# Encoder trunk on one core: operands of the first down steps made during the last gate/up pair, and a new order of the down products

## The chip, the cores and the metric

One core of a Trainium2 chip runs the whole program. The metric is the device time in microseconds (us), median of the runs; lower is better.

## What is computed

One layer of an encoder for 256 prompt and 1024 sample tokens (1280 together, width 1024): RMSNorm, an input projection, two groups of attention, an output projection added to the residual, and a feed-forward block. The change lies in the feed-forward block:

```
h2 = rmsnorm(x, ffn_norm_g)
x = x + (silu(h2 @ w_gate) * (h2 @ w_up)) @ w_down      # w_gate, w_up: 1024 x 2816; w_down: 2816 x 1024
y = rmsnorm(x, final_norm_g)
```

All is float32. TensorE multiplies in `float32r`, so every operand is split into a high part (a cast on ScalarE, called ACT in the profile) and a low part (raw minus high, on VectorE, DVE, or on GpSimd, POOL), and `mm3` issues three matmuls: high by high, high by low, low by high (lines 110 to 112).

## The kernel before

**Gate and up.** Both products are done block by block with seven products of half blocks instead of eight (a Strassen scheme). The tokens are in two halves of `NQ` = 640, the features in halves. Eleven pairs `fp` of output tiles are worked through; in each, first the gate (`i` = 0, into `G`), then the up part (`i` = 1, into `U`), each with the products `m` in the order `SEQ = (1, 2, 6, 7, 4, 5, 3)`. `S[m]` is the split activation operand of a product (TensorE's moving side, "S" and "zA" in the trace), made once for all pairs; `operand` makes the weight operand `wc` of each product (ACT and POOL, lines 849 and 850). `product` runs 24 matmuls of 320 columns, in two halves `s`, into the PSUM tiles `M0` and `M1`, and DVE adds each result into `G` or `U` (line 922). Products 2, 4 and 3 go on in the PSUM tile of the product ahead of them (`CHAIN`), once DVE has read it. `finish` applies Silu to a finished part of `G`, multiplies it into `U` (line 939), and makes the seven activation operands of the down projection (line 950), which are stored to `act_d[m][fp]` in DRAM. In the last pair these stores go through POOL's queue (`store_p`, line 70), in earlier pairs through ACT's.

**Down.** Again seven products, in the order `SEQ2`, each over `NH` = 11 steps `f`. A step needs an activation operand (loaded as `as` from `act_d[m][f]`, split into `ah`) and a weight operand (loaded as `w0_f` and `w1_f`, for the two halves of the columns; where `B_OP[m]` names two blocks they are first added or subtracted into `ws` on DVE, line 1065; then split into `w`). Both splits are `split_f`, lines 1025 (ACT) and 1026 (DVE). A step has 15 matmuls of 512 columns (5 token tiles by `mm3`) into the PSUM tiles `d`. After the last step of a product, `put` adds its five tiles into the output rows `x5` (`xs`, loaded from `xm_d`), one DVE instruction for each block that `D_OUT[m]` names (lines 1075 and 1077). `prepare`, `final` and `final_half` do the last RMSNorm.

**What sets the order.** SyncE's queue (SP), which issues all loads, keeps the order of the code; the other engines are ordered by a scheduler when the program is built. The down loop calls `bring` (loads) four steps ahead and `fetch` (splits) two steps ahead. Memory comes from stacks of pools: when the gate/up pools are released, the down pools take their place, and a tile in a reused place waits until the tile that was there has been read for the last time. Before, `x5` lay over the buffers `z` (the last pair's `G` and `U`), the raw down weights over `S7` and `S4`, the split weights `w` over `S6`.

## Time and profile before

| | us |
|---|---|
| median of 3 runs | 1669.48 |
| the runs | 1664.52, 1669.48, 1670.19 |
| the profiled execution, its own time | 1666.5 |
| its span, first to last instruction | 1664.5 |
| TensorE busy with matmuls | 1604.7 (96% of the span) |
| VectorE, ScalarE, GpSimd busy | 883.8, 716.7, 659.3 |
| mean granted TensorE clock | 0.992 |

The profile covers one execution. Its span runs from the first to the last instruction, and 2.0 us of that execution's time lie outside it. Gate and up end at 1376.5 us of the span, the down projection follows, and the last matmul begins at 1655.90. TensorE is busy nearly everywhere, so the places to look at are those where it waits or where its granted clock is under 1.00. In a timeline, the second number is how long an instruction (or a run of x equal ones) took; matmuls overlap, so the distance between two starts is what one costs.

### The profile page before, as it was taken

The page shows a single profiled execution, that of the slowest core. Times are in us where ns is not written, and L with a number is a line of the kernel's source. Part 1 is how long each engine was busy: PE and PEld are TensorE (multiplying, and loading weights), DVE is VectorE, ACT ScalarE, POOL GpSimd, SP SyncE. Part 2 cuts the span into 40 slices and gives each one's busy share as a digit, 9 for nine tenths or more (in the row PEclk, how much of TensorE's full clock was granted, in tenths as well). Part 3 has the DMA queues.
Part 4 walks back from the last instruction along what each step waited for, and adds up shares of the span by engine and source line. Part 5 has one row for each costly group of instructions (what it writes and reads, how often), then busy time and mean ns, then how long its engine had stood idle before and what let it go on. Part 6 is the DMA issues. An engine that isn't in the chain of part 4 may idle for free.

```text
span 1664.5 us, 25614 instructions
## 1 busy us (share of the span) xinstructions
PE 1604.7 (96%) x9601; PEld 1448.6 (87%) x9601; DVE 883.8 (53%) x1473; ACT 716.7 (43%) x1480; POOL 659.3 (40%) x803
## 2 busy tenths in 40 slices
PE   7999999999899999999989999999999999999998
PEld 6987899987688888788889999999999997788886
DVE  4654045455677777533464444334444437755776
ACT  5534145454577777544353222233223223333434
POOL 3451435354011119224677656565665550000101
PEclk9999999999999999999999999999999999999999
DMA  6635302225001003234302332232232228633434
GB/s 211 216 99 149 75 21 61 36 95 167 20 19 34 20 30 99 77 108 152 121 23 95 102 107 81 66 100 86 94 107 94 78 88 330 242 92 91 151 100 150
DMA packets 123212, 170.04 MB, mean 102 GB/s; under 512 B 35345, under 2 KB 66961, under 8 KB 123089
## 3 DMA queue, kind: packets, MB, share of 16 engines
q1 hardware_dynamic: 78848, 119.25, 23.0%
q10 hardware_dynamic: 43680, 46.87, 8.2%
q0 software_dynamic: 560, 2.29, 0.4%
q8 instruction: 75, 1.23, 0.3%
q14 instruction: 49, 0.39, 0.1%
HBM read 117.91 MB, written 50.46 MB: 101 GB/s over the span
## 4 chain that ended last, share of the span: by engine, by line
PE 82%; issue 4%; DMA 4%; DVE 4%; ACT 3%; POOL 3%; SPq 1%; ACTq 0%; POOLq 0%; DVEq 0%
PE M L110 11%; PE M L112 11%; PE M L111 11%; PE d L111 4%; PE d L112 4%; PE d L110 4%; PE o L686 3%; PE tp L679 3%; PE po L110 2%; PE po L111 2%; PE na_o L462 2%; PE po L112 2%; PE pj L110 2%; PE pj L112 2%; PE pj L111 2%
## 5 line engine op out<-in xcount | busy, mean ns | idle before, releaser
L110 PE MATMUL M<-S,wc 128*128 128x320 f32 x1056 | 322.4, 310 | 5.3 <-ACT wc L849 5.2
L111 PE MATMUL M<-S,wc 128*128 128x320 f32 x1056 | 324.9, 309 | 0.0
L112 PE MATMUL M<-S,wc 128*128 128x320 f32 x1056 | 313.2, 310 | 0.0
L110 PEld LDWEIGHTS M<-S,wc 128*128 128x128 f32 x1056 | 198.4, 189 | 5.9 <-ACT wc L849 5.8
L111 PEld LDWEIGHTS M<-S,wc 128*128 128x128 f32 x1056 | 199.3, 189 | 0.0
L112 PEld LDWEIGHTS M<-S,wc 128*128 128x128 f32 x1056 | 195.7, 189 | 0.6 <-POOL wc L850 0.6
L850 POOL TENSOR_TENSOR wc<-A,wc 128x512 fp32r<-128x512 f32 x86 | 119.5, 1391 | 83.6 <-ACT wc L849 83.2
L111 PE MATMUL d<-w,ah 128*128 128x512 f32 x385 | 147.1, 400 | 2.5 <-DVE w L1026 2.5
L110 PE MATMUL d<-w,ah 128*128 128x512 f32 x385 | 142.9, 400 | 2.7 <-ACT ah L1025 2.7
L112 PE MATMUL d<-w,ah 128*128 128x512 f32 x385 | 145.0, 400 | 0.0
L922 DVE TENSOR_TENSOR z<-M,z 128x320 f32<-128x320 f32 x120 | 56.9, 488 | 142.4 <-PE M L112 121.4
L849 ACT CAST wc<-A 128x512 fp32r<-128x512 f32 x86 | 53.5, 622 | 167.7 <-PE M L111 132.3
L850 POOL TENSOR_TENSOR wc<-sum,wc 128x512 fp32r<-128x512 f32 x62 | 88.3, 1425 | 86.6 <-ACT wc L849 81.5
L922 DVE TENSOR_TENSOR zB<-M,zB 128x320 f32<-128x320 f32 x100 | 47.6, 488 | 133.0 <-PE M L112 116.3
L100 DVE TENSOR_TENSOR PT<-tp,PT 128x512 fp32r<-128x512 f32 (+1 forms) x144 | 93.1, 658 | 41.1 <-ACT PT L99 39.7
L1025 ACT CAST ah<-as 128x640 fp32r<-128x640 f32 x77 | 56.0, 727 | 121.8 <-issue 61.9
L849 ACT CAST wc<-sum 128x512 fp32r<-128x512 f32 x62 | 38.4, 619 | 149.4 <-PE M L111 101.1
L99 ACT CAST PT<-tp 128x512 fp32r<-128x512 f32 (+1 forms) x144 | 79.2, 565 | 42.4 <-PE tp L679 39.4
L1026 DVE TENSOR_TENSOR ah<-as,ah 128x640 fp32r<-128x640 f32 x77 | 64.2, 836 | 53.9 <-ACT ah L1025 53.9
L110 PEld LDWEIGHTS d<-w,ah 128*128 128x128 f32 x385 | 73.2, 190 | 21.2 <-ACT ah L1025 3.4
L671 DVE TENSOR_REDUCE mm<-S 128x1 f32<-128x1024 f32 (+1 forms) x80 | 84.8, 1061 | 12.7 <-PE S L112 11.0
L111 PEld LDWEIGHTS d<-w,ah 128*128 128x128 f32 x385 | 73.1, 190 | 20.7 <-DVE w L1026 2.9
(398 smaller groups left out, 3978.0 us busy)
## 6 DMA issues: line engine op xcount, KB each, us to landing
as<-act_d SPq DMA_DIRECT2D x77, 320.0 KB
act_d<-z ACTq DMA_DIRECT2D x35, 320.0 KB
act_d<-zB ACTq DMA_DIRECT2D x35, 320.0 KB
A<-in_w_gate_dram SPq DMA_DIRECT2D x42, 256.0 KB
A<-in_w_up_dram SPq DMA_DIRECT2D x42, 256.0 KB
x<-in_x_tm_dram SPq DMA_DIRECT2D x20, 512.0 KB
cT_d<-stg ACTq DMA_DIRECT2D x20, 320.0 KB
w<-in_w_down_dram SPq DMA_DIRECT2D x11, 512.0 KB
```

Source lines behind the costliest of these rows:

```text
L99: i = nc.scalar.copy(out=hi, in_=ps)
L100: nc.vector.tensor_sub(out=lo, in0=ps, in1=hi)
L110: nc.tensor.matmul(out, lhsT=sh, rhs=mh, start=first, stop=False, **kw)
L111: nc.tensor.matmul(out, lhsT=sh, rhs=ml, start=False, stop=False, **kw)
L112: return nc.tensor.matmul(out, lhsT=sl, rhs=mh, start=False, stop=last, **kw).ins
L671: nc.vector.reduce_max(out=nm[:, u:u + 1], in_=S, axis=AX.X, negate=True)
L679: nc.tensor.transpose(tp[:, j], ex[:, kt * P:(kt + 1) * P], ident)
L849: i0 = nc.scalar.copy(out=hi, in_=raw)
L850: i1 = nc.gpsimd.tensor_tensor(out=lo, in0=raw, in1=hi, op=ALU.subtract)
L922: nc.vector.tensor_add(out=o, in0=ps, in1=a)
L1025: nc.scalar.copy(out=o[:, 0], in_=raw)
L1026: nc.vector.tensor_sub(out=o[:, 1], in0=raw, in1=o[:, 0])
```

## The change

- `S[1]` and `S[2]` become one tile each (`[P, 2, 4, NQ]`, high and low together) in the pool `rS`; the pool `rC` is gone, and `rS` is released at the very end.
- New: `down_first`, called in the last pair behind product 2 of the up part, when `S1` and `S2` are read for the last time. It takes their two places as rings, five slots for down weights (`w_ring`) and four for down activations (`a_ring`), and makes the operands of the first `EARLY` = 3 down steps in them: three weight tiles are loaded into buffers `A11`, `A12`, `A11` of the gate/up weights, three activation tiles into a buffer `zB`, and each is split by `split_f`.
- The down loop uses these rings for all steps (a fifth slot `ah` for the activations is new in `r5b`), skips what is made already, and has the order `SEQ2 = (5, 3, 1, 6, 2, 4, 7)` instead of `(3, 6, 1, 5, 2, 4, 7)`. Product 5 needs one weight block, `22`, and no sum.
- The output rows `xs` are loaded otherwise: five whole ones in product 5 (it writes only these), the halves of the other five in products 3 and 1. `gl_b` is loaded at the end of product 5, and `prepare` follows product 3.
- The pools `l5x`, `l5r` and those of the right side move: `x5` of row 0 now lies over `S6`, those of rows 1 to 5 over `z`, the raw down weights over `S5` and `S7`.
- In the first pair, `finish(G, U, i, 2, fp)` with the first Silu is called at `m == 4` instead of `m == 6`.

```diff
-    rC = pool("rC", side="right")
-    S = {1: [rS.tile([P, 4, NQ], F32R, name="S1", bufs=2) for x in "hl"],
-         2: [rC.tile([P, 4, NQ], F32R, name="S2", bufs=2) for x in "hl"]}
+    S = {}
+    for m in (1, 2):
+        x = rS.tile([P, 2, 4, NQ], F32R, name=f"S{m}")
+        S[m] = [x[:, 0], x[:, 1]]
...
+    def split_f(o, raw):
+        nc.scalar.copy(out=o[:, 0], in_=raw)
+        nc.vector.tensor_sub(out=o[:, 1], in0=raw, in1=o[:, 0])
+
+
+    NH = NF // 2
+    EARLY = 3
+    ops, w_ring, a_ring = {}, [], []
+
+    def down_first():
+        ring = rS.tile([P, 5, 2, 512], F32R, name="S1")
+        w_ring.extend(ring[:, n] for n in range(5))
+        ring = rS.tile([P, 4, 2, NQ], F32R, name="S2")
+        a_ring.extend(ring[:, n] for n in range(4))
+        z = rB.tile([P, 4, NQ], F32, name="zB", bufs=2)
+        for f in range(EARLY):
+            raw = rY.tile([P, 4, P], F32, name=("A11", "A12", "A11")[f],
+                          bufs=1 if f == 1 else 2).rearrange("p a b -> p (a b)")
+            load(raw, w_down[2 * f + 1 + NF])
+            load(z[:, f], act_d[5][f])
+            split_f(a_ring[f], z[:, f])
+            split_f(w_ring[f], raw)
+            ops[5, f] = a_ring[f], w_ring[f]
+
...
-                    if m == 6:
+                    if m == 4:
                         finish(G, U, i, 2, fp)
...
+                    if m == 2 and i == 1 and fp == NF // 2 - 1:
+                        down_first()
...
-    rC.release()
...
-    l5w, l5x, l5r = l5 = [pool("l5w"), pool("l5x"), pool("l5r")]
+    l5x, l5r = l5 = [pool("l5x"), pool("l5r")]
...
+    a_ring.append(r5b.tile([P, 2, NQ], F32R, name="ah"))
...
-        h = r5b.tile([P, 2, NQ], F32R, name="ah", bufs=5)
+        h = a_ring[steps.index((m, f)) % 5]
...
-        w = l5w.tile([P, 2, 512], F32R, name="w", bufs=5)
+        w = w_ring[steps.index((m, f)) % 5]
...
-    SEQ2 = (3, 6, 1, 5, 2, 4, 7)
+    SEQ2 = (5, 3, 1, 6, 2, 4, 7)
...
     def fetch(m, f):
-        ops[m, f] = act_operand(m, f), w_operand(m, f)
+        if (m, f) not in ops:
+            ops[m, f] = act_operand(m, f), w_operand(m, f)
...
-        load_a(m, f)
-        for n in (f - 2,) if 2 <= f < NH - 1 else (NT - 2, NT - 1) if f == NH - 1 else ():
-            if m == 3:
+        if (m, f) not in ops:
+            load_a(m, f)
+        if 2 <= f < 7 and m in (5, 3, 1):
+            n = f - 2 + (0 if m == 5 else 5)
+            if m != 1:
                 xs[n] = l5x.tile([P, D], F32, name="x5", bufs=10)
-                load(xs[n][:, 512:], xm_d[n][:, 512:])
-            elif m == 6:
-                load(xs[n][:, 0:512], xm_d[n][:, 0:512])
-        if m == 1 and f == 0:
+            cs = {5: slice(0, D), 3: slice(512, D), 1: slice(0, 512)}[m]
+            load(xs[n][:, cs], xm_d[n][:, cs])
+        if m == 5 and f == NH - 1:
             load(gl_b, g_fin.partition_broadcast(P))
...
-                if m == 5:
+                if m == 3:
                     prepare(t, ps[t])
...
+    rS.release()
```

The order of the instructions, as the program is built, is the same in both kernels on every engine up to the last pair. Three places show what that means. **The first Silu, on ACT**, in the first pair, before:

```order
L920 COPY z_9211<-M0_9286 128x320
L937 ACT_TABLE_LOAD
L937 ACTIVATE z_9210<-z_9210 128x640
L813 ACTIVATE zB_8005<-trm_9167,gf_8022 128x128 x4
L920 COPY z_9211<-M0_9272 128x320
```

And after the change:

```order
L921 COPY z_9206<-M0_9281 128x320
L938 ACT_TABLE_LOAD
L938 ACTIVATE z_9205<-z_9205 128x640
L814 ACTIVATE zB_8000<-trm_9162,gf_8017 128x128 x4
L921 COPY z_9206<-M0_9267 128x320
```

Only line and buffer numbers differ; the Silu and the table load ahead of it stand where they stood. **The last pair, on DVE**, from the evacuation of product 2 of the up part on, before (z_14074 is `G`, z_14075 is `U`, and M0_14425 and M1_14439 hold products 7 and 4):

```order
L922 TENSOR_TENSOR z_14075<-M0_14392,z_14075 128x320
L939 TENSOR_TENSOR z_14075<-z_14075,z_14074 128x640
L922 TENSOR_TENSOR z_14075<-M1_14406,z_14075 128x320
L922 TENSOR_TENSOR z_14075<-M0_14425,z_14075 128x320
L922 TENSOR_TENSOR z_14075<-M1_14439,z_14075 128x320
```

And after the change (z_14069 is `G`, z_14070 `U`, M0_14444 and M1_14458 hold products 7 and 4; S1_14378 and S2_14379 are the rings):

```order
L923 TENSOR_TENSOR z_14070<-M0_14411,z_14070 128x320
L968 TENSOR_TENSOR S1_14378<-A12_14388,S1_14378 128x512
L968 TENSOR_TENSOR S1_14378<-A11_14395,S1_14378 128x512
L923 TENSOR_TENSOR z_14070<-M1_14425,z_14070 128x320
L940 TENSOR_TENSOR z_14070<-z_14070,z_14069 128x640
L968 TENSOR_TENSOR S2_14379<-zB_14380,S2_14379 128x640 x2
L923 TENSOR_TENSOR z_14070<-M0_14444,z_14070 128x320
L968 TENSOR_TENSOR S2_14379<-zB_14380,S2_14379 128x640
L923 TENSOR_TENSOR z_14070<-M1_14458,z_14070 128x320
```

Four of the six early low parts now stand between the evacuation of product 2 and that of product 7's first half. On **SP** at the same place, after the change:

```order
L64 DMA A12_14388<-in_w_down_dram 128x512
L64 DMA zB_14380<-act5_d1_107 128x640
L64 DMA A11_14395<-in_w_down_dram 128x512
L64 DMA zB_14380<-act5_d2_108 128x640
L64 DMA w1_0_14605<-in_w_down_dram 128x512
L64 DMA w1_1_14607<-in_w_down_dram 128x512
L64 DMA w1_2_14609<-in_w_down_dram 128x512
L64 DMA x5_14611<-xm_d0_139 128x1024
L64 DMA w1_3_14613<-in_w_down_dram 128x512
L64 DMA as_14615<-act5_d3_109 128x640
L64 DMA x5_14617<-xm_d1_140 128x1024
L64 DMA w1_4_14619<-in_w_down_dram 128x512
```

The loads of steps 0 to 3 now stand ahead of x5_14617, the first load that goes into a place of `z`; before, x5_14602 in such a place stood behind the loads of steps 0 to 2 and ahead of those of step 3. **The end of the first down product, on DVE**, before (d_14640 to d_14644 are its results; w_14928 with ah_14923 is the operand of step 12, the second of the next product):

```order
L1065 TENSOR_TENSOR ws_14926<-w0_1_14863,w1_1_14594 128x512
L1026 TENSOR_TENSOR ah_14895<-as_14838,ah_14895 128x640
L1075 TENSOR_TENSOR x5_14602<-d_14640,x5_14602 128x512
L1075 TENSOR_TENSOR x5_14722<-d_14640,x5_14722 128x512
...
L1065 TENSOR_TENSOR ws_14964<-w0_2_14890,w1_2_14598 128x512
L1026 TENSOR_TENSOR ah_14923<-as_14865,ah_14923 128x640
...
L1075 TENSOR_TENSOR x5_14811<-d_14644,x5_14811 128x512
L1026 TENSOR_TENSOR w_14928<-ws_14926,w_14928 128x512
```

And after the change (ws_14839, ws_14865 and ws_14901 become the weights of steps 11, 12 and 13):

```order
L1086 TENSOR_TENSOR ws_14839<-w1_0_14605 128x512
L968 TENSOR_TENSOR S1_14378<-ws_14839,S1_14378 128x512
L1086 TENSOR_TENSOR ws_14865<-w1_1_14607 128x512
L968 TENSOR_TENSOR S2_14379<-as_14789,S2_14379 128x640
L1086 TENSOR_TENSOR ws_14901<-w1_2_14609 128x512
L968 TENSOR_TENSOR S2_14379<-as_14811,S2_14379 128x640
L968 TENSOR_TENSOR S1_14378<-ws_14865,S1_14378 128x512
L968 TENSOR_TENSOR S1_14378<-ws_14901,S1_14378 128x512
L1098 TENSOR_TENSOR x5_14611<-x5_14611,d_14625 128x512
L1096 TENSOR_TENSOR x5_14611<-d_14625,x5_14611 128x512
L968 TENSOR_TENSOR S2_14379<-as_14833,S2_14379 128x640
```

Before, the ten additions of `put` stood ahead of step 12's weight; now the weights of steps 11 to 13 stand ahead of all ten.

## Rows read from the trace of the kernel before

**Rows 1.** Page: one of three down groups; count, busy us, mean ns, idle before.

```profile
L111 PE MATMUL d<-w,ah 128*128 128x512 f32 x385 | 147.1, 400 | 2.5 <-DVE w L1026 2.5
```

**Rows 2.** Waits of TensorE, 1340 to 1664.5: us in total, times, longest.

```profile
PE d L110 <- ACT ah L1025: 2.7, 1, 2.7
PE d L111 <- DVE w L1026: 2.5, 1, 2.5
```

**Rows 3.** Timeline of TensorE: start us, us, instruction, idle before and releaser.

```profile
1376.34 0.31 PE L112 MATMUL M<-zA,wc 128*128 128x320 f32 x1
1379.33 0.51 PE L110 MATMUL d<-w,ah 128*128 128x512 f32 x1 [2.68 <-ACT ah L1025]
...
1384.48 1.34 PE L110 MATMUL d<-w,ah 128*128 128x512 f32 x5
...
1390.34 1.33 PE L112 MATMUL d<-w,ah 128*128 128x512 f32 x5
...
1424.38 0.40 PE L110 MATMUL d<-w,ah 128*128 128x512 f32 x1
1427.26 0.50 PE L111 MATMUL d<-w,ah 128*128 128x512 f32 x1 [2.48 <-DVE w L1026]
...
1432.40 0.39 PE L111 MATMUL d<-w,ah 128*128 128x512 f32 x1
...
1655.90 0.40 PE L112 MATMUL d<-w,ah 128*128 128x512 f32 x1
```

**Rows 4.** Windows: stretch, length, busy us of PE, PEld, DVE, ACT, POOL, clock, DMA, GB/s.

```profile
1380.00:1390.00 10.00, 10.00 (x38) 7.98 (x37) 5.99 (x10) 2.50 (x4) 1.08 (x2) 0.83 0.53 183
...
1384.50:1392.00 7.50, 7.44 (x32) 5.72 (x31) 3.49 (x6) 2.50 (x4) 0.00 (x0) 1.00 0.75 257
1400.00:1420.00 20.00, 20.00 (x87) 16.08 (x86) 13.13 (x20) 10.03 (x16) 0.00 (x0) 1.00 1.05 401
...
1429.60:1432.40 2.80, 2.80 (x9) 2.19 (x8) 2.80 (x5) 1.39 (x3) 0.00 (x0) 0.61 0.63 195
1432.40:1500.00 67.60, 67.60 (x290) 54.37 (x289) 43.57 (x65) 25.37 (x41) 0.00 (x0) 1.00 0.45 148
```

**Rows 5.** Timeline of DVE in the last pair and at the start of down.

```profile
1362.02 1.70 DVE L939 TENSOR_TENSOR z<-z 128x640 f32<-128x640 f32 x1 [2.08 <-ACT z L920]
...
1364.37 0.49 DVE L922 TENSOR_TENSOR z<-M,z 128x320 f32<-128x320 f32 x1 [0.25 <-PE M L112]
...
1368.48 0.49 DVE L922 TENSOR_TENSOR z<-M,z 128x320 f32<-128x320 f32 x1 [1.85 <-PE M L112]
...
1376.91 0.49 DVE L922 TENSOR_TENSOR z<-M,z 128x320 f32<-128x320 f32 x1
...
1380.03 0.82 DVE L1026 TENSOR_TENSOR ah<-as,ah 128x640 fp32r<-128x640 f32 x1
...
1389.71 0.69 DVE L1065 TENSOR_TENSOR ws<-w 128x512 f32<-128x512 f32 x1 [2.64 <-DMA w<-in_w_down_dram]
```

**Rows 6.** Timeline of POOL in the last pair.

```profile
1355.83 1.29 POOL L860 TENSOR_TENSOR sum<-A,sum 128x512 f32<-128x512 f32 x1
...
1361.74 1.30 POOL L850 TENSOR_TENSOR wc<-A,wc 128x512 fp32r<-128x512 f32 x1 [3.36 <-ACT wc L849]
```

**Rows 7.** Timeline of ACT in the last pair.

```profile
1361.04 0.62 ACT L849 CAST wc<-A 128x512 fp32r<-128x512 f32 x1 [2.69 <-PE M L111]
```

**Rows 8.** The chain that ended last, 1340 to 1440: start us, us, what.

```profile
1380.41 4.51 DMA act_d<-z
1385.06 0.33 SPq L64
```

**Rows 9.** DMA issues, 1340 to 1400: count, KB each, median us to landing.

```profile
act_d<-z POOLq DMA_DIRECT2D x7, 320.0 KB, 2.8
```

**Rows 10.** Timeline of DVE at the end of the first down product.

```profile
1419.19 3.68 DVE L1075 TENSOR_TENSOR x<-d,x 128x512 f32<-128x512 f32 x6 [2.49 <-PE d L112]
...
1426.51 0.69 DVE L1026 TENSOR_TENSOR w<-ws,w 128x512 fp32r<-128x512 f32 x1
```

More of the change, by code (lines that the diff above doesn't have):

```diff
@@ L1009, in encoder_trunk @@
     rY.release()
-    rS.release()
     pm[1].release()
     pm[0].release()
-    NH = NF // 2
     NLAST = 5
-    l5w, l5x, l5r = l5 = [pool("l5w"), pool("l5x"), pool("l5r")]
+    l5x, l5r = l5 = [pool("l5x"), pool("l5r")]
     r5a, r5b = r5 = [pool(nm, side="right") for nm in ("r5a", "r5b")]
@@ L1022, in encoder_trunk @@
     halves = r5a.tile([P, 5], F32, name="halves")
-    def split_f(o, raw):
-        nc.scalar.copy(out=o[:, 0], in_=raw)
-        nc.vector.tensor_sub(out=o[:, 1], in0=raw, in1=o[:, 0])
+    a_ring.append(r5b.tile([P, 2, NQ], F32R, name="ah"))
     B_OP = {1: ("11", ALU.add, "22"), 3: ("12", ALU.subtract, "22"), 6: ("11", ALU.add, "12"),
@@ L1112, in encoder_trunk @@
              7: (("11", 1),)}
-    SEQ2 = (3, 6, 1, 5, 2, 4, 7)
+    SEQ2 = (5, 3, 1, 6, 2, 4, 7)
     AHEAD, LOADED = 2, 4
     steps = [(m, f) for m in SEQ2 for f in range(NH)]
-    ops = {}
     def fetch(m, f):
-        ops[m, f] = act_operand(m, f), w_operand(m, f)
+        if (m, f) not in ops:
+            ops[m, f] = act_operand(m, f), w_operand(m, f)
     def bring(m, f):
         load_w(m, f)
-        load_a(m, f)
-        for n in (f - 2,) if 2 <= f < NH - 1 else (NT - 2, NT - 1) if f == NH - 1 else ():
-            if m == 3:
+        if (m, f) not in ops:
[3 more added lines that the diff above has]
+            if m != 1:
                 xs[n] = l5x.tile([P, D], F32, name="x5", bufs=10)
-                load(xs[n][:, 512:], xm_d[n][:, 512:])
-            elif m == 6:
-                load(xs[n][:, 0:512], xm_d[n][:, 0:512])
-        if m == 1 and f == 0:
+            cs = {5: slice(0, D), 3: slice(512, D), 1: slice(0, 512)}[m]
+            load(xs[n][:, cs], xm_d[n][:, cs])
+        if m == 5 and f == NH - 1:
             load(gl_b, g_fin.partition_broadcast(P))
```

## The prediction

> **What bounds the kernel now.** I read the page first: matmuls fill 96% of the span, so only places where TensorE waits or runs slowly can give time. The waits of TensorE behind 1340 us then show two, and only two, both in the down projection [rows 2]. The timeline of TensorE places them [rows 3]. The first is the change of stage: the last gate/up matmul starts at 1376.34, the first down matmul at 1379.33, held by the activation operand that ACT makes. The second is at 1424.38, where step 12, early in the second down product, waits 2.48 us for DVE to split its weight. The windows show what follows each: the granted clock is 0.83 over 1380 to 1390 and 0.61 over 1429.6 to 1432.4, against 1.00 later, so part of either stretch ran at 1.2 instead of 2.4 GHz; ahead of both TensorE stood still for some 2.5 us [rows 3, 4].
>
> **What undisturbed work would take.** From 1384.48 to 1390.34 there are five rows of five matmuls, so one costs 5.86 / 25 = 0.2344 us. Three groups of 385 [rows 1] are 1155 matmuls. Started without a gap at 1376.34 + 0.15 = 1376.49, the last would start 1154 x 0.2344 = 270.5 later, at 1647.0, and not at 1655.90: 8.9 us are in play. The parts: gap one 1379.33 - 1376.49 = 2.84; the first step's 15 matmuls took 5.15 instead of 3.52, 1.63 more; gap two 2.88 - 0.23 = 2.65; the 15 matmuls behind it 5.14 instead of 3.52, 1.62 more; 0.2 is scattered over steps 2 and 3. That is the most that this change can bring.
>
> **The change part by part.**
>
> *First Silu.* Nothing: the built order has it, with its table load, where it was. 0.
>
> *One tile for S1 and S2, other places, no pool rC.* Order and work up to the last pair are unchanged; 0.
>
> *Gap one.* Step 0 reads operands made some ten us ahead, so 2.84 goes, and with the standstill the slow stretch, 1.63. What could be late next is PSUM: the last evacuation of gate/up starts at 1376.91 and takes 0.49 [rows 5]. The built program puts the first five `d` tiles in other banks than this one, so I take 0; were one of them there, the second tile (needed 0.7 us after the start, at 1377.19) would wait some 0.3.
>
> *The early operands.* Added in the last pair: six loads, six casts on ACT, six low parts on DVE. DVE pays 3 x 0.69 (128x512, as in [rows 10]) + 3 x 0.82 (128x640 [rows 5]) = 4.5 us. The second weight tile goes into `A12`, which POOL reads until 1355.83 + 1.29 = 1357.1 [rows 6]; the nearest landing, 2.8 us for 320 KB [rows 9], puts it in SBUF at 1360. Its cast (some 0.62, as [rows 7]) is over before 1361.04, when the cast `wc` queued behind it on ACT ran anyway [rows 7]. The third cast follows at 1361.66 and its low part can start on DVE near 1362.3. There POOL is in its own subtraction, from 1361.74 to 1363.04 [rows 6], and DVE's line 939, started at 1362.02, took 1.70 instead of 0.82 [rows 5]: it ended 0.68 behind POOL's. So the low part ends near 1363.7; an evacuation (0.40), line 939 (0.74) and two more low parts (2 x 0.74) carry DVE to 1366.3, and the evacuation of product 7's first half, at 1364.37 before, ends at 1366.8. TensorE wants it for product 4, whose first half is evacuated at 1368.48 [rows 5]: less 12 matmuls of 0.1465 (0.2344 x 320 / 512) and some 0.2 it starts at 1366.5. So 0.3 to 0.4 us of waiting. Bounds: 0 if the low part misses POOL's instruction; 2.2 if both others are held 0.88 as well. I take 0.4, the walk along the rows.
>
> The Trainium skill (SBUF — State Buffer, Who interferes with whom) says that a DVE instruction with two SBUF inputs and a GpSimd instruction that reads SBUF lock each other out for a whole instruction. The 1.70 of line 939 agrees with it. By that rule each of the six low parts can be held, and the page speaks against putting them here; the sum above has one of them held, the second rival three, with its own time.
>
> *The SP queue.* The load of `x5` row 1 now goes into `U`'s place and waits for the last store of `act_d`; behind it stand the loads of step 4. Before, `x5` row 0 waited in the same way, until the store of 1380.41 had landed 4.51 later, at 1385.06 [rows 8], with step 3's loads behind it. In the change the three DVE instructions ahead of the last store follow the evacuation directly: 1376.91 + 0.40 + 3 x 0.83 + 0.3 to POOL = 1380.1; landing 2.8 [rows 9] to 4.5 later, so SP goes on at 1383.0 to 1384.8. Before, 768 KB behind such a release had landed 4.65 later (1385.06 to 1389.71, [rows 5, 8]); row 1's 512 KB and the 256 KB weight are the same 768 KB, and step 4's activations add 320 KB at 401 GB/s [rows 4], 0.8: in at 1388.5 to 1390.3, cast 0.8 later. Step 4 starts at 1376.49 + 60 x 0.2344 = 1390.55. So 0 to 0.6 late; with most landings near 2.8 I take 0.2. Steps 5 to 7 each load 1088 KB, 2.8 us at 401 GB/s, under a step's 3.52, so the delay doesn't grow. Over the whole first product the loads fall from 11 x (512 + 320) + 10 x 256 = 11,712 KB to 11 x 256 + 8 x 320 + 5 x 512 + 512 = 8,448 KB.
>
> *Gap two.* Product 5 has no `ws`: DVE's work for a step falls from 0.69 + 0.69 + 0.82 to 1.5 us. At its end the weights of steps 11 to 13 stand ahead of the ten additions. The next one behind them is step 14's: 10 x 0.61 (3.68 / 6, [rows 10]), 3 splits of activations (3 x 0.74), 2 `ws` and one split (3 x 0.61) are 10.2 us from the first addition; TensorE reaches step 14 three steps, 10.5 us, after the product's end. So 2.65 and 1.62 go, with little to spare; price if not, 4.3.
>
> *The rest.* `put`, `prepare`, `final` and the tail behind 1655.90 have the same instructions; `gl_b` comes earlier. 0. The scattered 0.2 goes too.
>
> **Sum.** 8.9 - 0.4 - 0.2 = 8.3. The span becomes 1664.5 - 8.3 = 1656.2, the profiled execution's 1666.5 becomes 1658.2. That execution lies 3.0 under the median; the four known executions average 1667.7. 8.3 off the median is 1661.2, off the average 1659.4; I predict **1660.3**.
>
> **Rivals.** *Gap two stays, or moves to a later product's end.* For it: 0.3 us of margin in the count above, and ten additions instead of the two-row ones of product 6 at more ends. Against: DMA, at 401 GB/s in 1400 to 1420 [rows 4], was what kept the operands only just ahead, and it has less to do. It gives back 4.3: 1660.3 + 4.3 = 1664.6.
>
> *DVE and POOL in the last pair.* If the low parts that stand ahead of product 7's evacuation are held like line 939 was, 0.88 each, TensorE waits 2.2 instead of 0.4, long enough for the slow stretch behind gap two: 1.8 + 1.6 more, 1663.7. For it the 1.70 in [rows 5]; against it, POOL has only one subtraction between 1361.7 and the store.
>
> *Slower: the loads of steps 4 to 7.* Each of these steps needs 1.11 MB. In 1380 to 1390 the queues moved 183 GB/s [rows 4]. If that were what they can do beside the stores, a step would take 6.1 us instead of 3.52: four steps lose 10.3, with two slow stretches of 1.6 13.5, and 8.3 - 13.5 gives 5.2 more than now, 1674.7. It turns into a loss below about 230 GB/s. Against it: 401 GB/s ten us later, and that the 183 contain SP's standstill until 1385.06.
>
> *The change doesn't do what it says.* True of the Silu (counted as 0). For the early operands the SP order shows their loads ahead of the down loads, so little is left: 1669.5.
>
> **Chances.** Forecast 64%, gap two 17%, DVE and POOL 9%, slower by the loads 5%, nothing gained 5%. A measurement of this kernel tells 0.5% from no change, 8.3 us: exactly the forecast's size. With the spread of the runs (1664.5 to 1670.2) I give five sixths of the forecast to faster, the rest and the next two rivals to the same: faster 0.54, same 0.40, slower 0.06. The range goes from the lowest run less 8.9, 1655.6, over the two rivals near 1664 up to 1667, their times with the runs' spread of 2 to 3.
>
> **What would show it.** Right: no wait between the last `M` and the first `d`, granted clock 1.00 over the first steps, the last `d` starting about 270.6 after the first, SP standing still at `x5` row 1 until about 1384. Wrong: a wait on DVE in the last pair of more than 0.5, on ACT at step 4, or on DVE behind a product's end; then the slow stretch behind it.

## The result, and the profile after

The changed kernel takes 1660.28 us (median of 15 runs, 1652.63 to 1664.00), the kernel before 1669.48 (15 runs beside them, 1664.52 to 1672.73): ratio 0.9941, 95% interval 0.9927 to 0.9954. The time came out where the prediction put it, 1660.3, but not by the sum that the prediction made. One term of that sum was twenty times too small, another that stood at 0 was the largest of all, and the two nearly cancel, so that the time was hit is luck. The experiments take them apart.

The profiled execution took 1656.26 us, its span 1654.4. The page's down group, which answers to [rows 1], has a new shape (activation operands in the ring `S` or in the fifth slot `ah`) and a shorter mean, 390 ns instead of 400:

```profile
L111 PE MATMUL d<-S,S 128*128 128x512 f32 x310 | 120.6, 390 | 0.0
```

The waits of TensorE behind 1340 us, in answer to [rows 2] (us in total, times, longest):

```profile
PE d L110 <- ACT ah L967: 2.8, 1, 2.8
PE M L110 <- DVE z L923: 0.4, 1, 0.4
PE M L110 <- ACT wc L850: 0.3, 1, 0.3
```

Both waits of before are gone. A new one of 2.8 us has come, and two small ones in the last gate/up pair. The timeline of TensorE, in answer to [rows 3], places the new one:

```profile
1377.41 0.31 PE L112 MATMUL M<-zA,wc 128*128 128x320 f32 x1
1377.56 0.39 PE L110 MATMUL d<-S,S 128*128 128x512 f32 x1
...
1390.05 1.29 PE L112 MATMUL d<-S,S 128*128 128x512 f32 x5
1394.15 0.50 PE L110 MATMUL d<-S,ah 128*128 128x512 f32 x1 [2.81 <-ACT ah L967]
...
1399.31 0.39 PE L110 MATMUL d<-S,S 128*128 128x512 f32 x1
...
1645.79 0.39 PE L112 MATMUL d<-S,S 128*128 128x512 f32 x1
```

Gate and up run straight into down (0.15 us apart), but step 4 waits. The windows, in answer to [rows 4] (stretch, length, busy us of PE, PEld, DVE, ACT, POOL, clock, DMA, GB/s):

```profile
1380.00:1390.00 10.00, 10.00 (x46) 8.29 (x45) 2.91 (x4) 1.35 (x2) 1.08 (x2) 1.00 0.72 278
...
1394.15:1398.00 3.85, 3.85 (x11) 3.02 (x12) 1.95 (x3) 1.34 (x2) 0.00 (x0) 0.65 1.04 393
```

The clock is 1.00 where it was 0.83, and 0.65 behind the new standstill: part of that stretch ran at 1.2 GHz.

**Account.** The instructions ahead of the first gate/up matmul are the same in both kernels, so I compare the stretch from that matmul to the last down matmul: 824.90 to 1655.90 before, 825.08 to 1645.79 after, 831.00 against 820.71 us, 10.3 less.

| | predicted | measured |
|---|---|---|
| gap one and the slow stretch behind it, scattered 0.2 | -4.7 | -4.7 |
| gap two and the slow stretch behind it | -4.3 | -4.3 |
| gate and up with the early operands | +0.4 | +0.9 |
| step 4 late | +0.2 | +4.6 |
| pace of the down matmuls | 0 | -6.9 |
| sum | -8.3 (from unrounded terms) | -10.4; the stretch says -10.3 |

Gate and up: first to last matmul 552.33 instead of 551.44. Step 4: 1394.15 less 1390.05 + 5 x 0.2267 is 2.97 of standstill, and its 15 matmuls took 5.16 instead of 3.49, 1.67 more. Pace: the undisturbed down matmuls average 0.2284 us instead of 0.2344, 1155 x 0.0060.

### The profile page after: what moved, and what is told of

It is laid out like the page before. It is cut to its first block, busy times and chain, and to the rows that moved or that the text cites. A ratio compares the mean times of both kernels' runs of the same rounds, so it can differ in the third digit from the quotient of the medians.

```text
span 1654.4 us, 25670 instructions
## 1 busy us (share of the span) xinstructions
PE 1597.0 (97%) x9601; PEld 1448.0 (88%) x9601; DVE 884.3 (53%) x1473; ACT 716.6 (43%) x1480; POOL 663.7 (40%) x803
## 4 chain that ended last, share of the span: by engine, by line
PE 83%; issue 4%; POOL 4%; DMA 3%; ACT 2%; DVE 2%; SPq 1%; POOLq 0%; ACTq 0%; DVEq 0%
PE M L112 10%; PE M L110 10%; PE M L111 10%; PE d L110 5%; PE d L112 5%; PE d L111 5%; PE o L686 3%; PE tp L679 3%; PE po L110 2%; PE po L111 2%; PE po L112 2%; PE pj L110 2%; PE pj L112 2%; PE pj L111 2%; PE na_o L462 2%
## 5 line engine op out<-in xcount | busy, mean ns | idle before, releaser
L111 PE MATMUL d<-S,S 128*128 128x512 f32 x310 | 120.6, 390 | 0.0
L110 PE MATMUL d<-S,S 128*128 128x512 f32 x310 | 118.6, 389 | 0.0
L112 PE MATMUL d<-S,S 128*128 128x512 f32 x310 | 117.2, 390 | 0.0
L699 POOL TENSOR_TENSOR ob<-ob 128x128 f32<-128x128 f32 x40 | 18.4, 461 | 177.0 <-ACT ob L696 176.9
L967 ACT CAST S<-as 128x640 fp32r<-128x640 f32 x59 | 42.9, 729 | 99.0 <-issue 60.1
L679 PE MATMUL tp<-ident,ex 128*128 128x128 f32 x544 | 79.8, 274 | 4.8 <-ACT ex L673 3.4
L686 PE MATMUL o<-PT,v 128*128 128x256 f32 x544 | 81.5, 288 | 1.6 <-ACT PT L99 1.4
```

The lines of the kernel that those rows point to most:

```text
L110: nc.tensor.matmul(out, lhsT=sh, rhs=mh, start=first, stop=False, **kw)
L111: nc.tensor.matmul(out, lhsT=sh, rhs=ml, start=False, stop=False, **kw)
L112: return nc.tensor.matmul(out, lhsT=sl, rhs=mh, start=False, stop=last, **kw).ins
L679: nc.tensor.transpose(tp[:, j], ex[:, kt * P:(kt + 1) * P], ident)
L686: nc.tensor.matmul(oT, lhsT=vv, rhs=pt[s][g][:, j], start=kt == 0 and s == 0, stop=kt == nkt - 1 and s == 1)
L967: nc.scalar.copy(out=o[:, 0], in_=raw)
```

## Why step 4 was late

The chain of the work that ended last shows it (start us, us, what):

```profile
1381.72 6.08 DMA act_d<-z
1387.94 0.33 SPq L64
1388.32 0.42 SPq L64
1388.84 4.46 DMA as<-act_d
1393.38 0.73 ACT ah L967
1394.15 0.50 PE d L110
```

SP's own queue shows the standstill: nothing between the load of step 3's activations and that of `x5` row 1.

```profile
1376.36 0.43 SPq L64 DMA_DIRECT2D as<-act_d  x1
1387.94 0.33 SPq L64 DMA_DIRECT2D x<-xm_d  x1
```

The prediction had this chain, and took its first two links too short: the last store was issued at 1381.72 and not 1380.1, and landed 6.08 us later and not 2.8 to 4.5. The third link it had right: step 4's activations were in 5.4 us behind SP's release at 1387.94, and 5.45 was predicted. So they came at 1393.3 and not at 1388.5 to 1390.3. The landing is the largest miss. Over the stores of this stretch it rose from a median of 2.9 to 7.0 us. What changed beside the stores is the loads: before, SP issued none between 1368.54 and 1385.06; now those of steps 0 to 3, which stand ahead of row 1, move at the same time. The two groups of DMA issues, 1374 to 1388, before and then after (KB each, us to landing):

```profile
act_d<-z POOLq DMA_DIRECT2D x6, 320.0 KB, 2.9
```

```profile
act_d<-z POOLq DMA_DIRECT2D x6, 320.0 KB, 7.0
```

and the loads in the same stretch, before and after (packets, MB, share of 16 engines):

```profile
q1 hardware_dynamic: 418, 0.83, 17.8%
```

```profile
q1 hardware_dynamic: 864, 1.90, 42.1%
```

Two of the runs below agree. With still more loads beside the stores (`rows_apart`, 2.74 MB in 1376 to 1390) their median is 8.3 us. In the run without early operands the four stores beside the loads have a median of 7.9, and the last one, issued when SP had started nothing for eight us, took 3.0.

**Experiment: the rows elsewhere.** Everything of the change is kept but the place of five output rows. The order of the instructions is the same on every engine.

```diff
-                xs[n] = l5x.tile([P, D], F32, name="x5", bufs=10)
+                xs[n] = l5x.tile([P, D], F32, name="x5" if n < 5 else "x6", bufs=5)
```

> The changed kernel with one thing moved: the five output rows of product 5 get a ring of their own over S6 (x5), the other five a ring over z (x6); the order of the instructions is the same on every engine. Theory one: TensorE's wait of 2.81 us at step 4 comes from SP, which stands at output row 1 from 1376.8 to 1387.9 until the last stores out of U have landed (6.08 us for the last one), with step 4's loads behind it. Rows over S6 don't wait for stores: SP goes on at once, no wait on ACT at step 4, granted clock 1.00 there, and the 2.9 of standstill and 1.9 of slow stretch go: span 1654.4 - 4.8 = 1649.6, last d starting 4.8 earlier against the first d. Theory two: the loads of step 4 are late because 1.1 MB a step and the seven stores share the queues, wherever the rows lie: the wait stays at 1 us or more, somewhere in steps 4 to 7, and the span at 1652 to 1655.

It takes 1654.62 us, ratio 0.9908 (0.9879 to 0.9936), and all that is left of the wait in down is

```profile
PE d L110 <- ACT ah L967: 0.2, 1, 0.2
```

First to last down matmul takes 264.09 us instead of 268.23, 4.1 less; the stretch of the account 817.10 instead of 820.71. So theory one holds: the place of the rows made SP wait for the stores, and 4.1 of the 4.8 come back. The profiled span fell less, to 1652.2 and not to 1649.6, because this execution reached its first gate/up matmul 1.4 us later and gate and up took 0.5 longer. What is missing of the 4.8 is theory two in small. SP now issues at once, and the loads pile up: in 1381 to 1393 the queues move 393 GB/s, and the activations of step 4 land 12.47 us after their issue, which makes step 4 0.2 us late.

```profile
1381.00:1393.00 12.00, 12.00 (x55) 9.86 (x53) 4.54 (x6) 2.24 (x4) 1.33 (x3) 1.00 0.99 393
```

## Why the down matmuls became faster

The trace of the changed kernel has a pattern that the prediction didn't foresee: four of five steps take 3.40 to 3.43 us (15 matmuls), the fifth, whose activation operand is in `ah`, 3.49. Before, all took 3.52. These are the first matmuls of four steps in a row, late in down:

```profile
1560.31 0.39 PE L110 MATMUL d<-S,S 128*128 128x512 f32 x1
...
1563.71 0.39 PE L110 MATMUL d<-S,S 128*128 128x512 f32 x1
...
1567.12 0.39 PE L110 MATMUL d<-S,ah 128*128 128x512 f32 x1
...
1570.61 0.39 PE L110 MATMUL d<-S,S 128*128 128x512 f32 x1
```

TensorE waits for nothing there, and its clock is 1.00. What goes by five is the slot, so the place of the operands was the suspect: of which operand, and which property of the place? Four runs of this section, the first two, the one of five more distances and the one of gate and up, are a single execution each (1665.79, 1660.34, 1660.89 and 1660.88 us) and are read for their paces alone.

**Experiment: the activation operand at other places.** The ring's slots are cut out of plain tiles at chosen offsets.

```diff
-        ring = rS.tile([P, 4, 2, NQ], F32R, name="S2")
-        a_ring.extend(ring[:, n] for n in range(4))
+        ring = rS.tile([P, 8 * NQ], F32R, name="S2")
+        a_ring.extend(ring[:, o:o + 2 * NQ].rearrange("p (a b) -> p a b", a=2)
+                      for o in (0, 2 * NQ + 8, 4 * NQ + 48))
...
-    a_ring.append(r5b.tile([P, 2, NQ], F32R, name="ah"))
+    low = r5b.tile([P, 4 * NQ + 56], F32R, name="ah")
+    a_ring.extend(low[:, o:o + 2 * NQ].rearrange("p (a b) -> p a b", a=2)
+                  for o in (0, 2 * NQ + 56))
```

> The changed kernel with the five slots of the activation operand (TensorE's stationary side) at other places; the weight slots (moving side) stay in the S1 ring. Slot 0: byte 208864 of the partition, 32 above a multiple of 64, as it was; slot 1: 214016, a multiple of 64; slot 2: 219296, 32 above; slot 3: 101920, 32 above, in the low region; slot 4: 107264, a multiple of 64, as it was. Step i uses slot i modulo 5, so one profile gives five paces. Theory A, alignment of the stationary operand: 0.2267 us for a matmul in slots 0, 2 and 3, 0.233 in slots 1 and 4. Theory B, region: 0.2267 in slots 0, 1 and 2, 0.233 in slots 3 and 4. Theory C, it is neither but something that goes with the fifth step (the load traffic, the scheduler's order): 0.2267 in slots 0 to 3, 0.233 in slot 4.

Matmuls 15 apart, from slot 0 to the next slot 0:

```profile
1562.29 0.40 PE L112 MATMUL d<-S,S 128*128 128x512 f32 x1
...
1565.72 0.40 PE L112 MATMUL d<-S,S 128*128 128x512 f32 x1
...
1569.21 0.39 PE L112 MATMUL d<-S,S 128*128 128x512 f32 x1
...
1572.65 0.40 PE L112 MATMUL d<-S,ah 128*128 128x512 f32 x1
...
1576.15 0.40 PE L112 MATMUL d<-S,ah 128*128 128x512 f32 x1
...
1579.64 0.40 PE L112 MATMUL d<-S,S 128*128 128x512 f32 x1
```

The steps take 3.43, 3.49, 3.44, 3.50 and 3.49 us. None of the three theories fits: slot 3 is slow though it lies 32 above a multiple of 64 (against A), slot 1 is slow in the upper region (against B), and three slots are slow, not one (against C).

**Experiment: the weight operand at other places.** The same for `w_ring`: offsets 0, 1032 and 2096 columns in `S1`, two slots in the lower region; the fifth activation slot goes into the rest of `S1`.

> The changed kernel with the five slots of the weight operand (moving side) at other places, and all five activation slots in the high region at 32 above a multiple of 64. Weight slot 0: byte 188384, 32 above a multiple of 64, as it was; slot 1: 192512, a multiple of 64; slot 2: 196768, 32 above; slot 3: 103968, 32 above, low region; slot 4: 108288, a multiple of 64, low region. Theory A, alignment of the stationary operand alone: 0.2267 us in all five slots. Theory A2, both operands must lie alike: 0.233 or 0.234 in slots 1 and 4. Theory B, region, of the moving operand too: slower in slots 3 and 4. Before, the moving operand was low, 32 above a multiple of 64, and the stationary one low and a multiple of 64: 0.2344.

The steps take 3.44, 3.50, 3.49, 3.44 and 3.49 us. Theory A falls (slots 1, 2 and 4 are slow), so does B (slot 3 is fast in the lower region), and A2 (slot 2 is slow, though both operands lie 32 above a multiple of 64).

What orders both runs is the distance: start of the stationary operand less start of the moving one, modulo 256 bytes. It is 0, 32, 192, 64 and 32 in the first run, 0, 224, 64, 192 and 224 in the second; 0 and 192 are fast in both, all others slow. Before it was 96. I call this theory D, and it was formed after these two runs, so it needed a test of its own.

**Experiment: the kernel before, shifted by 96 bytes.** One number, on a tile that has nothing to do with it:

```diff
-    halves = r5a.tile([P, 5], F32, name="halves")
+    halves = r5a.tile([P, 29], F32, name="halves")
```

> The kernel before with one number changed: the tile halves has 29 columns instead of 5, so the five activation operands ah lie 96 bytes lower, at 160 modulo 256 like the weight operands w; before they lay at 0. Nothing else changes, neither order nor amount of work. Theory D, from the paces of place_stationary and place_moving: the pace goes by the distance from the moving to the stationary operand modulo 256; 0 and 192 gave 0.2267 to 0.230, 32, 64 and 224 gave 0.232 to 0.2335, and before, at 96, it is 0.2343. So here, at 0, 0.227 to 0.230 in all steps: 1155 x 0.0045 to 0.0076 = 5 to 9 us less, ratio 0.995 to 0.997; both gaps stay. Rival, the rings' place in the upper region is what counts: 0.234 as before, ratio 1.000.

It takes 1659.15 us, ratio 0.9953 (0.9936 to 0.9970). Every undisturbed step takes 3.40 us:

```profile
1552.45 0.39 PE L110 MATMUL d<-w,ah 128*128 128x512 f32 x1
...
1555.85 0.39 PE L110 MATMUL d<-w,ah 128*128 128x512 f32 x1
```

and both gaps of before are still there:

```profile
PE d L110 <- ACT ah L1025: 3.2, 2, 2.7
PE d L111 <- DVE w L1026: 2.7, 1, 2.7
```

So 24 unused columns in the kernel before give nearly all of what the whole change gives: 0.9953 against 0.9941. The region is not the cause; these operands lie where they lay, but for 96 bytes.

**Experiment: five more distances.** The same slots as in the first experiment, at other offsets.

> The changed kernel with five distances of the stationary operand from the moving one, modulo 256: slots 0 to 4 at 128, 160, 192 (upper region), 96 and 0 (lower region). Theory D: slots 2 and 4 at 0.2267 to 0.230, slot 3 at 0.234 (the distance of before), 128 and 160 not measured yet. Rival, region: slots 3 and 4 slow, 0 to 2 fast.

The steps take 3.49 (128), 3.50 (160), 3.44 (192), 3.51 (96) and 3.44 us (0, in the lower region). Both named slots are fast, 96 is the slowest as before, region falls again. All eight multiples of 32 are measured now:

| distance modulo 256 | 0 | 32 | 64 | 96 | 128 | 160 | 192 | 224 |
|---|---|---|---|---|---|---|---|---|
| us per step of 15 | 3.40 to 3.44 | 3.49 | 3.49, 3.50 | 3.51, 3.52 | 3.49 | 3.50 | 3.44 | 3.49, 3.50 |

A fast step beside slow ones reads 3.43 or 3.44, one among fast ones 3.40; 192 was only measured beside slow ones.

**Experiment: the fifth slot at distance 0.** `rows_apart` with `halves` at 13 columns:

```diff
-    halves = r5a.tile([P, 5], F32, name="halves")
+    halves = r5a.tile([P, 13], F32, name="halves")
```

> The kernel rows_apart with the tile halves at 13 columns instead of 5, so the fifth activation slot lies 32 bytes lower, at distance 0 modulo 256 from its weight operand instead of 32. Theory D: the fifth slot's steps go from 0.2327 to 0.2267 to 0.229, 15 steps x 15 x 0.004 to 0.006, with what the steps beside them gain some 1 to 2 us less than rows_apart: about 1653. Rival, the fifth slot is slow because it lies in the lower region: no change, 1654.6.

It takes 1650.59 us, ratio 0.9898 (0.9876 to 0.9919); the fifth steps take 3.40, and first to last down matmul falls from 264.09 to 262.31 us. Theory D holds here too: 1.8 less, as expected.

**Experiment: gate and up.** Their matmuls have 320 columns and take 0.1467 us. The six buffers `wc` were put at three other distances.

```diff
-        hi = rY.tile([P, 4, P], F32R, name="wc", bufs=6)
-        lo = rY.tile([P, 4, P], F32R, name="wc", bufs=6)
+        if not wcs:
+            t = rY.tile([P, 6 * 512 + 128], F32R, name="wc")
+            wcs.extend(t[:, 512 * n + o:512 * n + o + 512].rearrange("p (a b) -> p a b", a=4)
+                       for n, o in enumerate((32, 32, 72, 72, 104, 104)))
+        hi, lo = wcs[0:2]
+        wcs[:] = wcs[2:] + wcs[0:2]
```

> The changed kernel with the three pairs of weight operands wc of gate and up at 128, 32 and 160 bytes further on modulo 256, used in turn by the products. The gate and up matmuls (320 columns) are at 0.1467 us, and their distances are 0 (products 1, 2, 3) and 64 (6, 7, 4, 5) now. Together with the products the three pairs give the distances 128, 192, 32, 96, 160 and 224. Theory D carried over to 320 columns: some of the blocks of 24 matmuls leave 0.1467, by up to 0.005 either way. Rival, these shorter matmuls don't go by the distance: 0.1467 in all blocks.

Next to nothing moves: where TensorE doesn't wait, the blocks of 24 lie between 0.1462 and 0.1472 us, against 0.1463 to 0.1467 in the changed kernel, and the groups' means stay at 309 to 310 ns. With 320 columns the distance makes at most 0.0005 us of difference, and none of the distances is faster than those in use; the 3696 matmuls of gate and up have nothing to gain from it.

Why the distance counts is open. The Trainium skill (SBUF — State Buffer, Who interferes with whom) lists two independent read ports of TensorE, one for the moving operand and one for loading weights, and says "PE and ACT never wait on anyone". The runs don't contradict the part on other engines. But the two sides of TensorE itself are not independent of each other here: the same 512-column matmul costs 0.2267 or 0.2343 us by nothing but the distance of its operands.

## What the early operands bring

**Experiment: without them.** The changed kernel with one number changed.

```diff
-    EARLY = 3
+    EARLY = 0
```

> The changed kernel with EARLY = 0: no operands are made in the last pair, all else is kept (rings, order of the products, places of the rows). Theory one: gap one comes back (about 2.8 us of wait on ACT before the first d, and a slow first step, 1.6 more), but it covers the lateness of step 4, whose loads go on when the last store has landed, near 1387, as before; and the last pair ends about 0.7 to 1.1 earlier. So the span stays within 2 us of 1654.4: in the changed kernel the early operands bring nothing yet. The pace of the d matmuls stays 0.2267 where the activation operand is in the S2 ring and 0.233 in the fifth slot. Theory two: step 4's wait is apart from gap one and comes on top: both are there, span near 1658.9.

It takes 1659.68 us, ratio 0.9944 (0.9926 to 0.9962), which the times don't tell from the changed kernel; by the stretch of the account it is 1.5 us slower (822.19 against 820.71). Neither theory has the reasons right. Gap one comes back as 0.97 instead of 2.99 us, and step 4's wait does not go, it grows:

```profile
1378.12 0.31 PE L112 MATMUL M<-zA,wc 128*128 128x320 f32 x1
1379.09 0.51 PE L110 MATMUL d<-S,S 128*128 128x512 f32 x1 [0.65 <-ACT S L967]
```

```profile
PE d L110 <- ACT ah L967: 4.0, 1, 4.0
PE d L110 <- ACT S L967: 0.8, 2, 0.7
```

The wait at step 4 grows because the last store is issued later. On DVE the low parts of steps 0 to 2 now stand among the last operands for `act_d`, and POOL issues the last store at 1387.80, where it was 1381.72 with early operands; SP went on right behind its landing, at 1390.97 instead of 1387.94.

```profile
1387.80 0.54 POOL L70 DMA_DIRECT2D act_d<-z  x1 [1.78 <-DVE z L951]
```

Two thirds of gap one, however, had gone without any early operand. The traces show why. Before, the first step's weight needed a sum (`ws`, DVE, at 1377.31), and ACT's cast waited for it until 1378.03. In the new order the first product is 5, which needs no sum; ACT's cast starts at 1377.37, as soon as the load is in, with gate and up still running. (This run keeps the new places too; what they do to gap one by themselves it doesn't show.) First the kernel before, then this one (ACT):

```profile
1378.03 0.62 ACT L1025 CAST w<-ws 128x512 fp32r<-128x512 f32 x1 [11.37 <-DVE ws L1065]
```

```profile
1377.37 0.62 ACT L967 CAST S<-w 128x512 fp32r<-128x512 f32 x1 [8.92 <-DMA w<-in_w_down_dram]
```

In exchange gate and up take 551.07 us instead of 552.33. The wait at step 4 hides the rest, so the same question was put to the mended kernels.

**Experiment: `rows_phase` with EARLY = 0.**

> rows_phase with EARLY = 0: what the early operands bring once step 4 is not late. Theory: gap one (2.8) and the slow stretch behind it (1.6) come back, the last pair gives back 0.7 to 1.1, so 3.3 to 3.7 us slower than rows_phase, ratio to before near 0.992. Rival: loads made in the last pair cost as much elsewhere as they save, within 1 us of rows_phase.

It takes 1656.29 us, ratio 0.9925 (0.9908 to 0.9941) against 0.9898, which looks like the theory. The traces say otherwise: first gate/up matmul to last down matmul is 815.42 us here and 815.49 with the early operands. The difference is ahead of that stretch, where both kernels have the same instructions: this execution reached its first `po` matmul at 701.6, the other at 693.5. It is not one odd execution: all four runs (1655.97 to 1657.00) lie above all four of `rows_phase` (1649.11 to 1652.04). What makes them later stays open. The windows of 120 to 180 and 360 to 480 show part of it, first of `rows_phase`, then of this one: the granted clock is 0.94 and 0.96 instead of 1.00 and 0.99, so more of that time ran at 1.2 GHz.

```profile
120.00:180.00 60.00, 54.66 (x270) 44.16 (x269) 21.08 (x44) 21.57 (x46) 11.95 (x23) 1.00 0.49 128
360.00:480.00 120.00, 106.47 (x651) 90.11 (x652) 72.88 (x155) 68.20 (x157) 37.09 (x70) 0.99 0.24 79
```

```profile
120.00:180.00 60.00, 55.12 (x261) 44.39 (x260) 21.71 (x45) 21.55 (x49) 11.46 (x26) 0.94 0.47 124
360.00:480.00 120.00, 106.52 (x631) 88.95 (x631) 69.61 (x159) 64.09 (x155) 40.46 (x71) 0.96 0.29 93
```

Trace and time disagreed, so the pair was run once more, on the last version.

**Experiments: the last version, with and without early operands.** `all_three` is `rows_phase` with the rows of product 5 loaded two steps later and, in the output projection, the stationary operand `mT` at distance 0 from `wo` instead of 64:

```diff
-    gm = rm.tile([P, KC], F32, name="gm")
+    gm = rm.tile([P, KC + 48], F32, name="gm")
...
-        if 2 <= f < 7 and m in (5, 3, 1):
-            n = f - 2 + (0 if m == 5 else 5)
+        if (4 if m == 5 else 2) <= f < (9 if m == 5 else 7) and m in (5, 3, 1):
+            n = f - 4 if m == 5 else f + 3
```

> rows_phase with two more things: the five rows of product 5 are loaded in its steps 4 to 8 instead of 2 to 6, and in the output projection the tile gm has 56 columns instead of 8, which puts the stationary operand mT at distance 0 modulo 256 from the moving wo instead of 64. Theory D: the po matmuls (512 columns) go from 0.2333 to 0.227 to 0.229, 480 x 0.0043 to 0.0063 = 2 to 3 us; the loads of steps 3 and 4 are no longer behind rows, which takes the 0.7 that steps 3 and 4 still lose in rows_phase (0.2647 and 0.236 instead of 0.2267 a matmul). Together 1647 to 1648, ratio 0.987 to 0.989. Rival: the distance counts only in the down stage, po stays at 0.2333, 1650.

> all_three with EARLY = 0. In the traces so far the stretch from the first gate and up matmul to the last down matmul is 815.49 us in rows_phase and 815.42 without the early operands, though the times gave 0.9898 and 0.9925; the trace of rows_phase_no_early had reached the first po matmul at 701.6 instead of 693.5, in a part of the program that both share. Theory one, early operands bring nothing net, they cost in gate and up (552.3 to 553.0 instead of 551.1) what they save at the start of down: the stretch is 814.4, as in all_three, within 1 us, and the ratio within the interval of all_three. Theory two, they bring the 4 to 5 us that the times showed: the stretch is 818 to 819, ratio near 0.992.

| | time us | ratio | first gate/up to last down matmul |
|---|---|---|---|
| all_three | 1650.30 | 0.9892 (0.9876 to 0.9907) | 814.37 |
| all_three, EARLY = 0 | 1652.16 | 0.9897 (0.9883 to 0.9911) | 814.58 |

They are the same, in time and in trace. With the early operands the start of down has no wait at all; without them it costs 0.98 us of gap and 0.5 in the first two steps, and gate and up are 1.1 us shorter (551.48 instead of 552.62). Theory one holds: once step 4 is not late, the early operands bring nothing net.

Of the two additions in `all_three` both did their work in the trace. The `po` matmuls fell from 0.2333 to 0.2282 us, a mean of 396 ns instead of 401, and the stretch from the first `po` to the first gate/up matmul from 129.8 to 127.6. The group's line of the kernel before, then of `all_three`:

```profile
L110 PE MATMUL po<-wo,mT 128*128 128x512 f32 x160 | 64.2, 401 | 0.7 <-ACT mT L99 0.7
```

```profile
L110 PE MATMUL po<-wo,mT 128*128 128x512 f32 x160 | 63.4, 396 | 0.7 <-ACT mT L99 0.7
```

First to last down matmul takes 261.60 us; 1154 undisturbed matmuls would take 261.6. The expected 2 to 3 us of time against `rows_phase` don't show in the ratio (0.9892, 0.9898): they are less than its interval, and this execution reached `po` 4.2 us later. `all_three` is 1.1% faster than the kernel before, and faster than the changed kernel, whose ratio is 0.9941; that it is faster than `rows_phase` isn't shown by the times. The 512-column matmuls `pj` lie at distance 64 and take 0.2327; shifting them wasn't tried.

## Why gap two went

**Experiment: ten rows in product 5.** `rows_phase`, but all ten output rows are loaded whole in product 5:

```diff
-        if 2 <= f < 7 and m in (5, 3, 1):
-            n = f - 2 + (0 if m == 5 else 5)
+        if m == 5 and f > 0:
+            n = f - 1
```

> rows_phase with all ten output rows loaded whole in product 5, one in each of its steps 1 to 10: the first product's loads rise from 8,448 to 11,008 KB, near the 11,712 of before. Theory of the prediction: gap two is gone because product 5 needs no ws and the weights of steps 11 to 13 stand ahead of its additions, so there is no wait at steps 11 to 14 here either. Rival: it is gone because fewer bytes are loaded; then TensorE waits 1 to 3 us somewhere in steps 8 to 14.

Gap two is back, at the same step 12 and of about the same size (one run, 1659.94 us; it also waits 1.1 and 0.5 us at steps 3 and 4):

```profile
1425.44 0.39 PE L110 MATMUL d<-S,S 128*128 128x512 f32 x1
1428.49 0.80 PE L111 MATMUL d<-S,S 128*128 128x512 f32 x1 [2.66 <-DVE S L968]
```

On DVE the low part of step 12's weight again stands behind the ten additions:

```profile
1426.56 0.68 DVE L1098 TENSOR_TENSOR x<-x,d 128x512 f32<-128x512 f32 x1
1427.16 0.68 DVE L1096 TENSOR_TENSOR x<-d,x 128x512 f32<-128x512 f32 x1
1427.76 0.68 DVE L968 TENSOR_TENSOR S<-ws,S 128x512 fp32r<-128x512 f32 x1
```

Product 5 needs no sum here either, so that alone doesn't remove the gap. With 11.0 MB of loads in the first product the operands come later: the sum for step 11's weight waits for its load and starts 4.1 us ahead of the first addition, against 6.9 in `rows_phase` with 8.4 MB, and the queues move 398 GB/s in 1400 to 1420 against 332. So the rival holds as far as this run goes: with the larger loads gap two is there. That the scheduler, when it builds the program, puts the additions first because the operands come later is my reading and not shown. The run changes both the bytes and the order on DVE, and it can't tell how much the order alone would do.

## Where the prediction was right and where it failed

- **Gap one, gap two and the slow stretches behind them:** the sizes hold (9.0 predicted and measured). Their causes only in part. The prediction gave gap one to operands made ten us ahead; two thirds of it go without them, in the new order that starts with product 5 and needs no sum. It gave gap two to the missing `ws` and to the weights standing ahead of the additions; without `ws` but with the larger loads neither that order nor the gain is there.
- **The early operands, 0.4:** 0.9 in this execution: 0.4 behind DVE, and 0.3 behind ACT's cast `wc`, which the walk left out (it stood behind the casts of the early operands). Against the runs without them gate and up pay 1.1 to 1.9 us, in the kernels where step 4 is not late as much as the early operands save behind. The 0.4 behind DVE has the size of the walk, but not its cause. The low part that the walk had held by POOL, from 1362.3, started at 1363.51, because its tile landed 4.96 us after its load was issued; it took 0.91 instead of 0.69 us. The one that was held longest, 1.50 instead of 0.82 beside POOL's subtractions from 1366.68 on, stands behind the evacuation for which TensorE waited:

```profile
1363.51 0.91 DVE L968 TENSOR_TENSOR S<-A,S 128x512 fp32r<-128x512 f32 x1 [0.81 <-ACT S L967]
...
1367.35 1.50 DVE L968 TENSOR_TENSOR S<-zB,S 128x640 fp32r<-128x640 f32 x1
```

  So the rule of the Trainium skill that the prediction weighed (SBUF — State Buffer, Who interferes with whom) agrees with this trace too, in two of the six low parts.
- **The SP queue, 0.2 (0 to 0.6):** the failing step. The chain was the right one, but the landing of the stores was taken from a stretch in which the loads of steps 0 to 2 had been issued eight us earlier. The change moved those loads beside the stores, and the landing rose from 2.9 to 7.0 us. It cost 4.6. The prediction named a wait on ACT at step 4 as a sign of error, and that is the sign that came.
- **"One tile for S1 and S2, other places: 0":** the other failing step. An undisturbed matmul was taken to cost 0.2344 wherever its operands lie. It costs 0.2267 at distance 0; the new places put four of five slots there, which the prediction did not look at. That is 6.9 us.
- **First Silu, 0:** the order on ACT is the same, and nothing in the trace speaks for a cost or a gain; it wasn't tried apart.
- **Rivals:** gap two didn't stay; DVE and POOL cost less than 2.2; the loads of steps 4 to 7 were late once, at the first step behind the standstill, and not in each.

The sum was 8.3 and the stretch gives 10.3: a miss of 4.4 and one of 6.9 the other way nearly cancel, and that is luck. With the pace left out the stretch would have given 3.4; by this account the change without its lucky places would have been worth about 0.2%.

## What to carry to other kernels

Before crediting a change with a gain, look at the time of one undisturbed instruction in both traces, and account for the stretch step by step: here a move of buffers changed the pace of 1155 matmuls, which no wait shows. Where a change puts more transfers beside a DMA on which something waits, take its landing time from a stretch as busy as the new one, not from the old. And where a tile lies over something that is still being stored, look at what is queued behind its load.

## What the runs showed of the hardware that was not expected

- A 512-column float32r matmul of the down projection takes 0.2267 us when the stationary operand starts at a distance of 0 modulo 256 bytes from the moving one, 0.2343 at 96, and between 0.229 and 0.234 at the other multiples of 32. In the output projection the step from 64 to 0 gave 0.2282 instead of 0.2333. For 320 columns no distance made more than 0.0005 us of difference (0.1462 to 0.1472).
- Executions of the same instructions reached the first `po` matmul between 693.5 and 701.6 us, with the granted clock of 120 to 180 at 1.00 in one and 0.94 in the other. Times of a few us are better compared over the stretch in which two kernels differ than over the whole.
